# Where the activations and low weights of layer 1 stand in memory: other row distance, other gap between high and low part, shifted low weights

## The chip, the core and the metric

The kernel runs on one core of one Trainium2 chip. The metric is the time on the device, in microseconds (us), of one launch. One execution is also recorded by the hardware profiler; its time is given beside its span, which is the time from the first to the last instruction.

The engines are named as in the profile: PE is TensorE's matmul, PEld its weight load, DVE is VectorE, ACT is ScalarE, POOL is GpSimd, SP is the engine that issues most of the DMAs.

## The reference

A decoder with two layers on 16 meta tokens and 256 sequence tokens (272 in all), width 2048, 16 heads of 128, feed-forward width 8192, all in fp32:

```python
h = concatenate([meta, x])                       # 272 tokens
# layer 0: forgetting attention
a = rms_norm(h, norm_attn[0]); q, k, v, f = split(a @ fox_w_in)
h = h + forgetting_attention(q, k, v, cumsum(log_sigmoid(f + b))) @ fox_w_o
h = h + square(relu(rms_norm(h, norm_mlp[0]) @ w_up[0])) @ w_down[0]
# layer 1: stick-breaking attention over a shared K/V
k_s, v_s = split(rms_norm(h, kv_norm) @ w_kv)
q = rms_norm(h, norm_attn[1]) @ sb_w_q
h = h + stick_breaking_attention(q, k_s, v_s) @ sb_w_o
h = h + square(relu(rms_norm(h, norm_mlp[1]) @ w_up[1])) @ w_down[1]
return rms_norm(h, final_norm)[16:]
```

Nearly all the arithmetic is in the products with weight matrices: 96 blocks of 512 output features over 2048 input features, each.

## The kernel before

**Three products for one.** Activations are held feature-major: 128 partitions, 16 chunks of 128 features, and the tokens along the free axis. To keep fp32 accuracy with the faster float32r matmuls, every operand is split into a high part (rounded to float32r) and a low part (the rest). A product is then high x high + high x low + low x high, summed in PSUM.

**Activations.** `Split` (from line 119) makes a tile of 16 rows for one activation, one row for each chunk, with the high and the low part of the chunk in one row. The table `ROWS` (line 28) says, in words of 4 bytes, how far rows are apart, where the high part begins and where the low part begins. For layer 0, where all 272 tokens are needed (`t0` = 0), rows are 640 words (2560 bytes) apart, the high part begins at 48 (byte 192) and the low part at 368 (byte 1472). For layer 1 after the shared K/V (`t0` = 16, 256 tokens) rows are 576 words (2304 bytes) apart, the high part begins at word 16 (byte 64) and the low part follows right behind it at 272. `both` is the two parts of a row as one operand of 512 columns; it is used in layer 1 alone, since 2 x 272 columns do not fit into the 512 of one PSUM bank.

**Weights.** `gemm_group` (from line 182) multiplies one block of 512 output features. It goes over four quarters `kb` of the input features. For each it loads four chunks of weights (issued on SP's queue, two chunks to a DMA), and for each half of them line 217 makes the high weights `whi` on ScalarE and line 218 the low weights `wlo` on VectorE. There are four buffers of each. The tile `pad` of 128 bytes (line 115) puts the weight buffers, and the activation tiles behind them, at multiples of 256 bytes.

**Matmuls.** All are issued through `gemm_matmul` (from line 174), line 176 in the profile. Without `pairs` (layer 0 and the shared K/V) there are three matmuls of 272 columns for each chunk and each 128 output features: `whi` with high, `whi` with low, `wlo` with high. With `pairs` (layer 1's query and output projections and its MLP) there are two: `whi` with `both`, 512 columns, and `wlo` with the high part, 256 columns. In the first and last quarter the four output features' blocks come one after the other (four 512s, then four 256s); in the two middle quarters two chunks go with all four blocks (eight 512s, then eight 256s). A manual dependency from each matmul to the one before it pins this order, so no scheduler changes it. In one group of layer 1 there are 64 of each; there are 40 such groups, and in the last one a quarter of the products is done in the form of layer 0 (256 columns).

Lines 600 to 605 are matmuls of the stick-breaking attention, float32r as well, whose activations come in two pieces: 2 x 256 or 2 x 144 columns with a jump between them. Lines 305 and 306 multiply layer 0's activations with the 16 forget-gate weights (high and low, 32 columns).

Of the kernel before, what the change touches and what calls it, by code (L numbers as in the profile page):

```python
# [10 lines left out]
F32R = mybir.dt.float32r  # L11
# [4 lines left out]
P = 128  # L16
D = 2048
NC = D // P
M = 16
# [4 lines left out]
QSCALE = 1.0 / math.sqrt(P)  # L24
N_FF = 4


ROWS = {0: (640, 48, 368), M: (576, 16, 272)}
XROW = 640

G_A0, G_M0, G_KV, G_A1, G_M1, G_FIN = range(6)
# [3 lines left out]
def yoco_kernel(ctx: ExitStack, tc: tile.TileContext, hT_in, gains, b_f, w_f, w_qkv0, w_o0, w_up, w_dn,  # L35
# [7 lines left out]
    wspl = ctx.enter_context(tc.tile_pool(name="wspl", bufs=4))  # L43
# [75 lines left out]
    class Split:  # L119


        def __init__(self, label, t0):
            n = T - t0
            self.t0 = t0
            rows = xs.tile([P, NC * XROW + 64], F32R, tag="x", name=f"x_{label}")
            pitch, hi, lo = ROWS[t0]
            rows = rows[:, hi:hi + NC * pitch].rearrange("p (c t) -> p c t", c=NC)
            self.hi, self.lo = rows[:, :, :n], rows[:, :, lo - hi:lo - hi + n]
            self.both = rows[:, :, :2 * n]

    def split_chunk(sp, gi, c):

# [41 lines left out]
    def gemm_matmul(*args, **kw):  # L174

        ins = nc.tensor.matmul(*args, **kw).ins  # L176
        if queued and pinned[0]:
            tc.add_manual_dep(ins, queued[0].name, mybir.DependencyInfo(mybir.DependencyClass.NoSync,
                                                                        mybir.DependencyReason.DATA))
        queued[:] = [ins]  # L180

    def gemm_group(wblk, sp, t0, evac, before={}, after={}, load_x=None, pairs=False, apart=()):

        uid[0] += 1
        u = uid[0]
        accs = [pacc.tile([P, 512], F32, tag="acc", name=f"acc_{u}_{m}") for m in range(4)]  # L190
        n = T - t0
        for kb in range(4):
            src_w = wblk[kb].rearrange("p (k c) -> p k c", k=4)
            if kb in before:
                before[kb]()
            piece = 1 if load_x is not None and kb < 2 else 2
            raws = [wraw.tile([P, 2, 512], F32, tag="raw", name=f"raw_{u}_{kb}_{hf}") for hf in range(2)]
            for k0 in range(0, 4, piece):
                if load_x is not None:
                    load_x(range(4 * kb + k0, 4 * kb + k0 + piece))  # L200
                if load_x is not None and kb == k0 == 0:

                    for c0 in (0, 256):
                        nc.scalar.dma_start(raws[0][:, 0, c0:c0 + 256], src_w[:, 0, c0:c0 + 256])
                else:
                    nc.sync.dma_start(raws[k0 // 2][:, k0 % 2:k0 % 2 + piece], src_w[:, k0:k0 + piece])
            parts = []
            for hf in range(2):
                whi = wspl.tile([P, 2, 512], F32R, tag="whi", name=f"whi_{u}_{kb}_{hf}")
                wlo = wspl.tile([P, 2, 512], F32R, tag="wlo", name=f"wlo_{u}_{kb}_{hf}")  # L210
                boxes = [(o, piece, 0, 512) for o in range(0, 2, piece)]
                if load_x is not None and kb == hf == 0:
                    boxes[:1] = [(0, 1, 0, 256), (0, 1, 256, 512)]
                for o, no, c0, c1 in boxes:
                    src = raws[hf][:, o:o + no, c0:c1]
                    hp, lp = whi[:, o:o + no, c0:c1], wlo[:, o:o + no, c0:c1]
                    on_act = nc.scalar.activation(hp, src, AF.Copy)  # L217
                    on_dve = nc.vector.tensor_tensor(out=lp, in0=src, in1=hp.bitcast(F32), op=ALU.subtract)  # L218
                parts.append((whi, wlo))
            if kb in after:  # L220
                with tc.issue_after(on_act.ins), tc.issue_after(on_dve.ins):
                    after[kb]()


            if load_x is not None and kb == 0:
                runs = [([kc], range(4)) for kc in range(4)]
            elif kb in (0, 3):
                runs = [(range(4), [m]) for m in range(4)]
            else:
                runs = [(range(2 * hf, 2 * hf + 2), range(4)) for hf in range(2)]  # L230
            pinned[0] = load_x is None
            for kcs, ms in runs:
                paired = [m for m in ms if pairs and m not in apart]
                single = [m for m in ms if m not in paired]
                for kc in kcs:
                    for m in paired:
                        gemm_matmul(accs[m], parts[kc // 2][0][:, kc % 2, m * P:(m + 1) * P], sp.both[:, 4 * kb + kc],
                                    start=kb == kc == 0, stop=False)
                for kc in kcs:
                    for m in paired:  # L240
                        gemm_matmul(accs[m][:, :n], parts[kc // 2][1][:, kc % 2, m * P:(m + 1) * P],
                                    sp.hi[:, 4 * kb + kc], start=False, stop=kb == kc == 3)
                for m in single:
                    for kc in kcs:
                        wh, wl = (w[:, kc % 2, m * P:(m + 1) * P] for w in parts[kc // 2])
                        hi, lo = sp.hi[:, 4 * kb + kc], sp.lo[:, 4 * kb + kc]
                        gemm_matmul(accs[m][:, :n], wh, hi, start=kb == kc == 0, stop=False)
                        gemm_matmul(accs[m][:, :n], wh, lo, start=False, stop=False)
                        gemm_matmul(accs[m][:, :n], wl, hi, start=False, stop=kb == kc == 3)
                if kb == 3:  # L250
                    for m in ms:
                        evac(m, [accs[m][:, :n]] + ([accs[m][:, n:]] if m in paired else []))
# [18 lines left out]
    def load_x(chunks):  # L271
        c0, n = chunks[0], len(chunks)
        nc.sync.dma_start(hT[:, c0:c0 + n, :], hT_in[:, c0:c0 + n, :])
        if c0 == 0:
            nc.sync.dma_start(g_sb, gains)
        for c in chunks:
            split_chunk(xa, G_A0, c)
# [86 lines left out]
    for g in range(4):  # L364
# [11 lines left out]
        if g == 0:  # L376

            gemm_group(w_qkv0[0], xa, 0, lambda m, acc, qT=qT: nc.scalar.copy(qT[:, m, :], acc[0]),
                       after={kb: (lambda kb=kb: first_norm(kb)) for kb in range(4)}, load_x=load_x)
            gate_products()  # L380
            box["rstd"] = norm.finish()
            for m in range(4):
                evac_q(m, [qT[:, m, :]])
            forget_gates(box["rstd"])
        else:
            gemm_group(w_qkv0[3 * g], xa, 0, evac_q)
# [4 lines left out]
        def decays(j):  # L391

            for i, (o, n) in enumerate(((0, 144), (144, T))):
                nc.vector.scalar_tensor_tensor(out=s[:, j, o:o + n], in0=fk[:, j, :n],
                                               scalar=fq_sb[:, i, 4 * g + j:4 * g + j + 1],
                                               in1=maskA[:, o:o + n], op0=ALU.subtract, op1=ALU.add)

        gemm_group(w_qkv0[3 * g + 1], xa, 0, lambda m, acc: evac_kv(m, acc, kT),
                   after={j: (lambda j=j: decays(j)) for j in range(4)})

# [255 lines left out]
    a, y, t, rs = (fin[:, i, :] for i in range(4))  # L656
# [81 lines left out]
```

## Time and profile before

| | before |
|---|---|
| time, median of 3 runs | 2323.51 us (2322.72 to 2324.66) |
| profiled execution | 2323.63 us, span 2321.9 us |
| granted TensorE clock | 0.998 |
| PE busy | 2310.8 us (100%), 16486 instructions |
| DVE, ACT busy | 1350.6 us (58%), 1064.0 us (46%) |
| DMA | 412.00 MB, 177 GB/s on average |

Matmuls are pipelined: the next one starts before the one ahead has ended. The duration that the profile gives for one is therefore longer than the step from its start to the start of the next, and it is the steps that add up to the time.

### The profile page before, as it was taken

To read this page: it belongs to the slowest core of one execution; us is meant where nothing else is said; L and a number is where in the kernel's file an instruction comes from. 1 tells how busy PE (TensorE), PEld (TensorE's weight loads), DVE (VectorE), ACT (ScalarE), POOL (GpSimd) and SP (SyncE) were. 2 spreads that over 40 slices of the span, in tenths; PEclk is the share of its full clock that TensorE was granted. 3 is DMA by queue.
4 is the path that set the end of the run, shared out by engine and by line. 5 is a ranking of instruction groups with operands and counts; after the bars stand their busy time and mean duration, and the time that the engine had idled before them with its cause. 6 is when DMAs were issued, how large, how long until landed. Compare 5 with 4: busy or idle time off the path is not lost.

```text
span 2321.9 us, 39954 instructions
## 1 busy us (share of the span) xinstructions
PE 2310.8 (100%) x16486; PEld 2190.4 (94%) x16486; DVE 1350.6 (58%) x1923; ACT 1064.0 (46%) x1477; POOL 39.9 (2%) x58
## 2 busy tenths in 40 slices
PE   9999999999999999999999999999999999999998
PEld 9999999999999999999998999988888888888887
DVE  7665555655455455445566655567665665665665
ACT  6434344544344344344455444455544543543553
POOL 1000000000000000000000000000000000000000
PEclk9999999999999999999999999999999999999999
DMA  6544444455555455555556444455555555556553
GB/s 233 172 156 165 171 158 173 171 183 173 183 175 183 171 186 176 178 182 171 187 173 200 155 145 146 146 175 186 197 184 193 192 186 198 186 184 199 181 199 127
DMA packets 116630, 412.00 MB, mean 177 GB/s; under 512 B 13264, under 2 KB 16736, under 8 KB 116448
## 3 DMA queue, kind: packets, MB, share of 16 engines
q1 hardware_dynamic: 114560, 406.29, 51.4%
q10 hardware_dynamic: 1888, 3.16, 0.4%
q8 instruction: 129, 2.11, 0.4%
q14 instruction: 53, 0.43, 0.1%
HBM read 407.29 MB, written 2.11 MB: 176 GB/s over the span
## 4 chain that ended last, share of the span: by engine, by line
PE 99%; DMA 0%; DVE 0%; ACT 0%; issue 0%; DVEq 0%; SPq 0%; ACTq 0%
PE acc L176 95%; PE ps L406 0%; PE pza L585 0%; PE pv L339 0%; PE po L468 0%; PE po L624 0%; DMA raw<-w_qkv 0%; PE po L625 0%; PE pzb L586 0%; PE po L469 0%; DMA hT<-hT_in 0%; PE po L626 0%; DVE ob L680 0%; PE pf L306 0%; PE pf L305 0%; PE pta L600 0%
## 5 line engine op out<-in xcount | busy, mean ns | idle before, releaser
L218 DVE TENSOR_TENSOR wlo<-raw,whi 128x1024 fp32r<-128x1024 f32 (+1 forms) x773 | 931.5, 1217 | 746.8 <-ACT whi L217 745.2
L217 ACT ACTIVATE whi<-raw 128x1024 fp32r<-128x1024 f32 (+1 forms) x773 | 799.2, 1050 | 953.9 <-PE acc L176 877.4
L176 PE MATMUL acc<-x_u,whi 128*128 128x272 f32 (+2 forms) x3088 | 647.5, 321 | 0.0
L176 PE MATMUL acc<-x_m,whi 128*128 128x272 f32 (+1 forms) x3072 | 646.1, 322 | 0.0
L176 PEld LDWEIGHTS acc<-x_u,whi 128*128 128x128 f32 x3088 | 499.9, 188 | 26.7
L176 PEld LDWEIGHTS acc<-x_m,whi 128*128 128x128 f32 x3072 | 497.8, 188 | 27.4
L176 PE MATMUL acc<-x_u,wlo 128*128 128x272 f32 (+1 forms) x2048 | 445.9, 282 | 0.0
L176 PE MATMUL acc<-x_m,wlo 128*128 128x272 f32 (+1 forms) x2048 | 443.7, 282 | 0.0
L176 PE MATMUL acc<-x_a,whi 128*128 128x272 f32 (+1 forms) x1792 | 360.6, 306 | 0.4 <-ACT x_a L134 0.2
L176 PEld LDWEIGHTS acc<-x_u,wlo 128*128 128x128 f32 x2048 | 340.3, 188 | 15.7
L176 PEld LDWEIGHTS acc<-x_m,wlo 128*128 128x128 f32 x2048 | 339.5, 188 | 15.9
L176 PEld LDWEIGHTS acc<-x_a,whi 128*128 128x128 f32 x1792 | 284.4, 188 | 9.9 <-issue 0.7
L176 PE MATMUL acc<-x_a,wlo 128*128 128x272 f32 (+1 forms) x1024 | 254.5, 286 | 0.0
L176 PE MATMUL acc<-x_kv,whi 128*128 128x272 f32 x1024 | 194.1, 288 | 0.0
L176 PEld LDWEIGHTS acc<-x_a,wlo 128*128 128x128 f32 x1024 | 179.6, 188 | 4.9 <-issue 0.5
L176 PE MATMUL acc<-x_o,whi 128*128 128x272 f32 (+1 forms) x768 | 162.3, 322 | 0.0
L176 PEld LDWEIGHTS acc<-x_kv,whi 128*128 128x128 f32 x1024 | 160.6, 188 | 0.4
L176 PE MATMUL acc<-x_kv,wlo 128*128 128x272 f32 x512 | 147.3, 288 | 0.0
L256 DVE TENSOR_TENSOR hT<-acc,hT 128x256 f32<-128x256 f32 (+1 forms) x239 | 102.4, 428 | 71.4 <-PE acc L176 69.5
L176 PEld LDWEIGHTS acc<-x_o,whi 128*128 128x128 f32 x768 | 124.3, 188 | 6.8
L176 PE MATMUL acc<-x_o,wlo 128*128 128x272 f32 (+1 forms) x512 | 111.6, 283 | 0.0
L176 PEld LDWEIGHTS acc<-x_kv,wlo 128*128 128x128 f32 x512 | 96.5, 188 | 0.1
(226 smaller groups left out, 1040.0 us busy)
## 6 DMA issues: line engine op xcount, KB each, us to landing
raw<-w_up SPq DMA_DIRECT2D x256, 512.0 KB, 4.7
raw<-w_dn SPq DMA_DIRECT2D x256, 512.0 KB, 4.7
raw<-w_qkv SPq DMA_DIRECT2D x92, 512.0 KB, 3.8
raw<-w_o SPq DMA_DIRECT2D x64, 512.0 KB, 4.5
raw<-w_kv SPq DMA_DIRECT2D x64, 512.0 KB, 3.6
raw<-w_q SPq DMA_DIRECT2D x32, 512.0 KB, 4.6
fk<-f_dram ACTq DMA_DIRECT2D x4, 544.0 KB, 5.0
raw<-w_qkv SPq DMA_DIRECT2D x7, 256.0 KB, 4.8
```

The lines of the kernel that those rows point to most:

```text
L176: ins = nc.tensor.matmul(*args, **kw).ins
L217: on_act = nc.scalar.activation(hp, src, AF.Copy)
L218: on_dve = nc.vector.tensor_tensor(out=lp, in0=src, in1=hp.bitcast(F32), op=ALU.subtract)
L256: nc.vector.tensor_tensor(out=hT[:, c, t0:], in0=a, in1=hT[:, c, t0:], op=ALU.add)
```

## The change

Rows of all activations are 640 words (2560 bytes) apart, layer 1's too. In layer 1 the high part begins at byte 0 of its row, a multiple of 256, and the low part 304 words (1216 bytes) behind it, so that 192 bytes lie unused between the two and `both` is an operand of two pieces. The tiles of split weights grow from 2 x 512 to 2 x 576 words; in layer 1 (`pairs`) the low weights are put 16 words (64 bytes) into their tile. The two halves of a weight tile thus lie 2304 instead of 2048 bytes apart, in both layers. No instruction is added or taken away on any engine, and their order is the same.

```diff
-ROWS = {0: (640, 48, 368), M: (576, 16, 272)}
+ROWS = {0: (48, 368), M: (0, 304)}
 XROW = 640
...
             rows = xs.tile([P, NC * XROW + 64], F32R, tag="x", name=f"x_{label}")
-            pitch, hi, lo = ROWS[t0]
-            rows = rows[:, hi:hi + NC * pitch].rearrange("p (c t) -> p c t", c=NC)
-            self.hi, self.lo = rows[:, :, :n], rows[:, :, lo - hi:lo - hi + n]
-            self.both = rows[:, :, :2 * n]
+            hi, lo = ROWS[t0]
+            rows = rows[:, hi:hi + NC * XROW].rearrange("p (c t) -> p c t", c=NC)
+            d = lo - hi
+            self.hi, self.lo = rows[:, :, :n], rows[:, :, d:d + n]
+
+            self.both = rows[:, :, :2 * d].rearrange("p c (i t) -> p c i t", i=2)[:, :, :, :n]
...
-                whi = wspl.tile([P, 2, 512], F32R, tag="whi", name=f"whi_{u}_{kb}_{hf}")
-                wlo = wspl.tile([P, 2, 512], F32R, tag="wlo", name=f"wlo_{u}_{kb}_{hf}")
+                whi, wlo = (wspl.tile([P, 2, 576], F32R, tag=f"w{x}", name=f"w{x}_{u}_{kb}_{hf}") for x in ("hi", "lo"))
+                whi, wlo = whi[:, :, :512], wlo[:, :, 16:528] if pairs else wlo[:, :, :512]
```

## The prediction

> **What bounds the kernel now.** I read the page's busy table first, then the waits of TensorE, the chain of work that ended last, and the timeline of TensorE in layer 1.
>
> ```profile
> PE 2310.8 (100%) x16486; PEld 2190.4 (94%) x16486; DVE 1350.6 (58%) x1923; ACT 1064.0 (46%) x1477; POOL 39.9 (2%) x58
> PE 99%; DMA 0%; DVE 0%; ACT 0%; issue 0%; DVEq 0%; SPq 0%; ACTq 0%
> PE acc L176 95%; PE ps L406 0%; PE pza L585 0%; PE pv L339 0%; PE po L468 0%; PE po L624 0%; DMA raw<-w_qkv 0%; PE po L625 0%; PE pzb L586 0%; PE po L469 0%; DMA hT<-hT_in 0%; PE po L626 0%; DVE ob L680 0%; PE pf L306 0%; PE pf L305 0%; PE pta L600 0%
> ```
>
> TensorE is busy throughout and 95% of the chain is the matmuls of line 176. So the time is the number of matmuls times the distance from one start to the next. The "mean ns of one" in the page (393 for 512 columns) is longer than that distance, because matmuls overlap; distances have to be read from start times. The chain's long pieces give them:
>
> ```profile
> 442.52 757.05 PE acc L176 x6112
> ...
> 1610.15 693.91 PE acc L176 x4020
> ```
>
> The first piece is layer 0, where every matmul has 272 columns: 757.05 / 6112 = 123.9 ns each. The second is layer 1, where matmuls of 512 columns (high weights on both halves of a row) and of 256 (low weights on the high half) come in equal numbers: 172.6 ns on average. The timeline separates the two (start, length in us; the next row's start minus this one's, divided by the count, is the distance):
>
> ```profile
> 1798.40 1.09 PE L176 MATMUL acc<-x_m,whi 128*128 128x512 f32 x4
> 1799.33 0.62 PE L176 MATMUL acc<-x_m,wlo 128*128 128x256 f32 x4
> ...
> 1803.94 2.00 PE L176 MATMUL acc<-x_m,whi 128*128 128x512 f32 x8
> 1805.78 1.10 PE L176 MATMUL acc<-x_m,wlo 128*128 128x256 f32 x8
> 1806.72 2.00 PE L176 MATMUL acc<-x_m,whi 128*128 128x512 f32 x8
> 1808.56 1.11 PE L176 MATMUL acc<-x_m,wlo 128*128 128x256 f32 x8
> 1809.51 2.00 PE L176 MATMUL acc<-x_m,whi 128*128 128x512 f32 x8
> 1811.34 1.07 PE L176 MATMUL acc<-x_m,wlo 128*128 128x256 f32 x8
> 1812.25 1.99 PE L176 MATMUL acc<-x_m,whi 128*128 128x512 f32 x8
> ```
>
> Runs of 512 columns stand 230 (1.84 / 8), 230, 228.8 ns apart, and 232.5 in the run of four. Runs of 256 stand 117.5, 118.8 and then 113.8 ns apart. The same instruction on the same kind of data takes two speeds, without an idle moment. That is the only thing in this profile which a change of addresses alone could move.
>
> **What changes, and what does not.** On every engine the built program has the same instructions in the same order as before; only addresses and the shape of three operands differ. Nothing is removed and no wait is added. Byte positions within 256 are what I call residues; weight and activation tiles start at residue 0 in both kernels.
>
> *Layer 0* keeps its rows (2560 bytes apart, both parts at residue 192). Its weight tiles grow from 4096 to 4608 bytes, so the second half lies 2304 instead of 2048 bytes on, still residue 0. In the runs above, activations move by 2304 bytes and weights by 512 with no visible step, so I put this at nothing. If it did matter, 10,752 matmuls would pay: 1 ns each is 10.8 us.
>
> *The weight splits* (lines 217 and 218) write two pieces of 512 instead of one of 1024. Bound: nothing, up to two separate pieces, from these rows:
>
> ```profile
> L217 ACT ACTIVATE whi<-raw 128x1024 fp32r<-128x1024 f32 x764 | 794.0, 1055 | 950.1 <-PE acc L176 877.4 <-DVE hT L256 54.1 <-DMA fqm_sb<-f_dram 6.1
> L217 ACT ACTIVATE whi<-raw 128x512 fp32r<-128x512 f32 x7 | 4.4, 624 | 1.5 <-DMA raw<-w_qkv 1.5
> ```
>
> That is 2 x 624 - 1055 = 193 ns at most on ScalarE, eight times per group of 128 matmuls (22.17 us, start 1798.40 to the next group at 1820.57): 1.5 us, while ScalarE sits idle 877 us in all because it waits for TensorE to free weight buffers. Hidden. Without that cover it would be 764 x 0.19 = 147 us.
>
> *Layer 1's low part* moves from right behind the high part to 1216 bytes behind it. The 512-column operand becomes two pieces of 256 with a jump between. There are 2544 such matmuls (the by-form rows: 1024 + 1008 + 256 + 256). Only the stick-breaking matmuls of lines 600 to 605 already read two pieces:
>
> ```profile
> 1322.50 0.39 PE L601 MATMUL pta<-el,ntri_r 128*128 128x512 f32 x1
> 1322.73 0.30 PE L602 MATMUL pta<-eh,nones_r 128*128 128x288 f32 x1
> 1322.86 0.30 PE L603 MATMUL pta<-el,nones_r 128*128 128x288 f32 x1
> 1323.00 0.30 PE L605 MATMUL ptb<-el,ntri_r 128*128 128x288 f32 x1
> 1323.13 0.42 PE L176 MATMUL acc<-x_kv,whi 128*128 128x272 f32 x2
> ```
>
> Their pieces start at residues that neither version of the rows uses. Three matmuls of 2 x 144 columns take 400 ns (1322.73 to 1323.13), 133.3 each. In one piece, 288 columns should take 123.9 plus 16 columns at (230 - 116.4) / 256 = 0.44 ns, or 130.9. So a jump costs about 2.4 ns. Line 601, 512 columns in two pieces, takes 230 ns, like the contiguous ones: a jump for nothing. Upper end: line 600's 240 ns (1320.53 to 1320.77 in the same timeline), 10 ns over 230. I take 2.4, from three in succession, and keep 0 and 10: 2544 x 2.4 = +6.1 us (0 to +25).
>
> *The residues of layer 1* go from 64 for everything on the activation side and 0 for weights to: high activations 0, low activations 192, high weights 0, low weights 64. For the 256-column matmuls the activations now stand 64 before the weights, modulo 256 the same difference (192) that layer 0 has throughout. Layer 0's 123.9 ns for 272 columns, less 16 x 0.44, is 116.9 for 256; layer 1's mean now is 116.4 (the group's 22.17 us is 64 x 346.4, less 64 x 230). So for these 2592 matmuls I expect +0.5 ns, within the rounding: 0. The bounds are the fastest and slowest runs seen, 113.8 and 118.8: -6.7 to +6.2 us. For the 512s the runs of four in this stretch span 227.5 (1799.79 to 1800.70) to 232.5: -6.4 to +6.4 us, taken at 0 because no row has activations and weights at one residue.
>
> A rule of the Trainium skill speaks against any effect of the weights' place: "TensorE: Matmul & The Clock Gate", Part 2, says that matmul operand and weight load have independent read ports and don't take bandwidth from each other. The trace bears it out where weights are small: lines 305 and 306 load 32 columns instead of 128, and ten of them take 1.25 us (31.69 to 32.94), 125 ns each against 123.9 with full weights. By that rule the residue term is zero, and the sum has the jump alone.
>
> **Sum.** The profiled execution took 2323.63 us (span 2321.9, 1.7 around it), 0.1 above the median of 2323.51. 2323.6 + 6.1 = 2329.7, say **2330**. A measurement of this kernel can tell about 0.2% (4.6 us) from no change.
>
> **The rivals.**
>
> *Faster: the new residues put every run on its fast speed.* For: the two speeds exist at one and the same instruction and shape, so what decides is how activations' and weights' reads fall against each other, and the change sets that anew in each of the three pairings. Against: layer 0's residues differ from layer 1's and cost the same per column. All 256s at 113.8 and all 512s at 227.5: 2592 x 2.6 + 2544 x 2.5 = 13.1 us, 2310; it shows as faster once it beats the jump by 4.6 us. Chance 0.30. The same page gives N / 2.4 + 2.5 ns as the bare distance between matmuls; an estimate by it, 215.8 and 109.2 ns, would make the most that could be gained 55 us.
>
> *No difference.* The jump is free, as in line 601, and the residues do nothing: 2323 to 2325. Also the case if lock-in at the two speeds is reached whatever the addresses. Chance 0.15.
>
> *Much slower: equal residues collide.* Now high activations and high weights both start at residue 0, which no matmul of line 176 has in the kernel before. If each 512 meets the next weight load head on, the nearest price is line 600's 10 ns: 25 us; with all 256s at 118.8, another 6: 2349 to 2355. It becomes decisive above 4 ns per matmul. Chance 0.20.
>
> *The forecast*, jump paid and residues about even, 2328 to 2338: 0.35.
>
> **Numbers.** Faster by over 0.2% is 0.30; within 0.2% is the second rival, 0.15; slower is 0.35 + 0.20 = 0.55. The range runs from 2309, just below the gain of 13, to 2348, which leaves out the farther part of the collision and any gain beyond the fast speeds. Cases of both signs hold most of it; the forecast's own range is 2328 to 2338.
>
> **What would show it.** Right: the 512-column runs of layer 1 stand 2 to 3 ns farther apart, the 256s near 116 to 117, layer 0's chain piece still gives 123.9, TensorE has no new idle time. The residues matter if runs of 256 come all at one speed. The forecast is wrong if the 512s fall below 229, if layer 0 moves, or if ScalarE's wait for TensorE shrinks to nothing.

## The result, and the profile after

The changed kernel takes 2316.13 us (2315.55 to 2316.42), the kernel before 2323.47 us in the same series: ratio 0.9968, 95% interval [0.9956, 0.9979]. It is faster by 7.3 us, where I forecast 6.5 us slower. The time lies inside the stated range, in the part of it that the first rival holds; the forecast itself missed the sign.

The page of the changed kernel, busy times (line 176 is now line 177):

```profile
PE 2303.4 (100%) x16486; PEld 2183.1 (94%) x16486; DVE 1350.1 (58%) x1923; ACT 1064.1 (46%) x1477; POOL 40.8 (2%) x58
```

TensorE is as full as before and issues as many instructions; it is busy 7.4 us less. The chain's long pieces say in which layer:

```profile
442.66 756.95 PE acc L177 x6112
...
1608.68 688.23 PE acc L177 x4020
```

Layer 0's piece was 757.05 us and is unchanged. Layer 1's was 693.91 and is 5.7 us shorter. The rest of the gain is in layer 1's shorter pieces. The timeline of TensorE in the same group of layer 1 (start, length in us):

```profile
1795.29 1.08 PE L177 MATMUL acc<-x_m,whi 128*128 128x512 f32 x4
...
1800.78 2.00 PE L177 MATMUL acc<-x_m,whi 128*128 128x512 f32 x8
1802.62 1.07 PE L177 MATMUL acc<-x_m,wlo 128*128 128x256 f32 x8
1803.53 2.00 PE L177 MATMUL acc<-x_m,whi 128*128 128x512 f32 x8
...
1817.26 1.08 PE L177 MATMUL acc<-x_m,whi 128*128 128x512 f32 x4
```

A run of eight 512s takes 1800.78 to 1802.62, 230 ns each, as before. A run of eight 256s takes 1802.62 to 1803.53, 113.8 ns each by these rounded starts; by the unrounded ones of the trace 113.3, and so in all but three of the layer's 469 runs of 256. Before, a third of the runs stood at 113.3 by unrounded starts and the others at 117.5 to 118.5, and the mean was 116.4. The whole group takes 1795.29 to 1817.26, 21.97 us instead of 22.17. Forty groups at 0.2 us are 8 us, about the result.

The weight splits are still hidden, and ScalarE still waits for TensorE nearly as long as before (873.8 us in its row for line 218, against 877.4).

### The profile page after: what moved, and what is told of

Same layout as the page of the kernel before. It is cut to its first block, busy times and chain, and to the rows that moved or that the text cites. A ratio compares the mean times of both kernels' runs of the same rounds, so it can differ in the third digit from the quotient of the medians.

```text
span 2314.5 us, 39954 instructions
## 1 busy us (share of the span) xinstructions
PE 2303.4 (100%) x16486; PEld 2183.1 (94%) x16486; DVE 1350.1 (58%) x1923; ACT 1064.1 (46%) x1477; POOL 40.8 (2%) x58
## 4 chain that ended last, share of the span: by engine, by line
PE 99%; DVE 0%; DMA 0%; ACT 0%; issue 0%; SPq 0%; DVEq 0%; ACTq 0%
PE acc L177 96%; PE ps L407 0%; PE pza L586 0%; PE pv L340 0%; PE po L469 0%; PE po L625 0%; PE pzb L587 0%; PE po L626 0%; PE po L470 0%; DMA g_sb<-gains 0%; PE po L627 0%; DVE ob L681 0%; PE pf L306 0%; PE pf L307 0%; PE pta L601 0%; PE pta L602 0%
## 5 line engine op out<-in xcount | busy, mean ns | idle before, releaser
L218 ACT ACTIVATE whi<-raw 128x1024 fp32r<-128x1024 f32 (+1 forms) x773 | 799.1, 1050 | 948.0 <-PE acc L177 873.8
```

## The experiments

What had to be explained: why the 256s all run at 113.3 ns now, and why the 512s' mean didn't move although they got a jump and new starts. All starts below are in bytes modulo 256. "Speed" is the distance from the start of one matmul to that of the next. Where the text names two rows it is worked out from their rounded starts, which is good to about 1 ns in a run of eight and 2.5 ns in a run of four; elsewhere, and in all means, it is from the unrounded starts of the trace.

The theories as they stood when the first runs were made: **A**, that the difference between the start of the activations and that of the low weights decides (192, where it was 64); **B**, that a start of the high activations at a multiple of 256 decides; **C**, that the 512s ahead, with their jump, leave TensorE in a state that decides how the 256s go.

### One part of the change alone

The changed kernel without the displacement of the low weights:

```diff
-                whi, wlo = whi[:, :, :512], wlo[:, :, 16:528] if pairs else wlo[:, :, :512]
+                whi, wlo = whi[:, :, :512], wlo[:, :, :512]
```

> The changed kernel with its rows (2560 bytes apart, high part at residue 0, low part at 192), but the low weights back at residue 0. Theory A (the 256-column matmuls run at their fast speed when the high activations stand 192 past the low weights, modulo 256): the difference is now 0, so runs of 256 fall back to a mixture near 116.4 ns and the time to about 2323 us. Theory B (the start of the activations at a multiple of 256 decides, whatever the weights): all runs of 256 stay at 113.3 ns, about 2316 us. Theory C (the 512s ahead, with their jump, leave TensorE in a state that decides): also 113.3 ns and 2316 us.

Measured: 2332.88 us, ratio to the kernel before 1.0039 [1.0024, 1.0054]. Its timeline in layer 1:

```profile
1809.39 1.12 PE L177 MATMUL acc<-x_m,wlo 128*128 128x256 f32 x8
1810.35 2.00 PE L177 MATMUL acc<-x_m,whi 128*128 128x512 f32 x8
```

The 256s stand 120 ns apart (1809.39 to 1810.35; 119.4 in the mean of the layer), where the slow runs of the kernel before had 118.5 at most; the 512s are nearly where they were, at 230.6 in the mean. So 64 bytes on the low weights, in this setting, are worth 16.8 us. All three theories missed: A expected a mixture near 116.4 ns, B and C expected 113.3. B falls, and so does C in the form above, since the 512s kept their starts and their jump. What is left of it is a wider **C**, which the later runs test: the matmuls ahead leave TensorE's reads in a position that is kept, so that the 512s' starts have a part in the 256s' speed, beside the 256s' own.

The other part alone, the kernel before with low weights displaced by 64:

```diff
-                wlo = wspl.tile([P, 2, 512], F32R, tag="wlo", name=f"wlo_{u}_{kb}_{hf}")
+                wlo = wspl.tile([P, 2, 576], F32R, tag="wlo", name=f"wlo_{u}_{kb}_{hf}")
+                wlo = wlo[:, :, 16:528] if pairs else wlo[:, :, :512]
```

(the tile of `whi` grows likewise, and is used from its start).

> The kernel before with its rows (2304 bytes apart, both parts at residue 64 and contiguous), and the low weights of layer 1 displaced by 64 bytes; weight tiles as in the change. Theory A: the difference of high activations and low weights becomes 0 instead of 64, not 192: no gain of 7 us, somewhere within 2320 to 2330. Theories B and C: nothing changes, 2323.5 us, runs of 256 at 113.8 to 118.8 as before. If it gives 2316, the weights' place alone is the cause.

Measured: 2326.62 us, 1.0014 [1.0004, 1.0023]. Activations and low weights now both start at 64, and over half of the 256s go at 119 to 121 ns, some at 113; the mean is 117.8. Equal starts are slow in both runs, but here not for all. A had 2320 to 2330 us for this run, B and C no change.

### The same difference, no jump

High part at 192 and the low part right behind it, low weights at 0: A's difference of 192 without a jump.

```diff
-ROWS = {0: (48, 368), M: (0, 304)}
+ROWS = {0: (48, 368), M: (48, 304)}
-                whi, wlo = whi[:, :, :512], wlo[:, :, 16:528] if pairs else wlo[:, :, :512]
+                whi, wlo = whi[:, :, :512], wlo[:, :, :512]
```

> Rows of layer 1 2560 bytes apart, high part at residue 192 and the low part right behind it (no jump), low weights at residue 0. The difference of activations and weights is 192 for all three pairings, as in layer 0. Theory A: runs of 256 all at 113.3 ns, about 2316 us. Theory B: mixed as before, 2323 us. Theory C: no jump, mixed as before, 2323 us.

Measured: 2324.83 us, 1.0005 [0.9996, 1.0014]. In its timeline

```profile
1804.37 2.02 PE L177 MATMUL acc<-x_m,whi 128*128 128x512 f32 x8
1806.23 1.07 PE L177 MATMUL acc<-x_m,wlo 128*128 128x256 f32 x8
1807.15 2.02 PE L177 MATMUL acc<-x_m,whi 128*128 128x512 f32 x8
```

the 256s do go at 113.3 (all but the first of a run, which brings their mean to 114.3), as A had it, but the 512s take 232.5 ns (1804.37 to 1806.23; mean 232.4) instead of 230, and eat the gain. No theory had that: A expected 2316 us, and B and C, whose 2323 us is near, expected the 256s mixed as before. The version without a jump is the slower, but its starts differ too, so this run doesn't price the jump; two of the sweeps below do.

### A sweep of starts, matmuls alone

```python
for rh, rl, rw in product(range(4), repeat=3):   # starts of high part, low part, low weights
    # twice: eight 512s (whi, both parts), then eight 256s (wlo, high part)
```

> Not the decoder: only matmuls on copies of inputs, in runs of 24 to 48, with their places swept (letters a to p are starts 0, 16, ... 240 bytes past a multiple of 256; o, a, b, c are 0, 64, 128, 192), and the output is a copy of the input. Lines by group: 256 columns by start; 256 columns by start and by the weights' start; 272 columns; 512 contiguous; layer 1's pattern of eight 512s and eight 256s by starts of high part, low part and low weights; layer 0's pattern of three by the same. Theory A: in the 256-column groups the distance depends on the difference alone, 113.3 ns at 192. Theory B: it depends on the activations' start alone. Theory C: groups of 256 alone all have one speed, and in the pattern it depends on the low part's start. If neither place matters, all groups of a shape have one distance: 116.4, 123.9, 230.

The names of its groups give the three starts, o, a, b and c for 0, 64, 128 and 192. Three groups with the high part at 0:

```profile
261.12 1.11 PE L90 MATMUL pair_ooa<-x,wl 128*128 128x256 f32 x8
262.06 2.00 PE L85 MATMUL pair_ooa<-x,wh 128*128 128x512 f32 x8
...
325.63 1.12 PE L90 MATMUL pair_oco<-x,wl 128*128 128x256 f32 x8
326.59 2.00 PE L85 MATMUL pair_oca<-x,wh 128*128 128x512 f32 x8
328.43 1.07 PE L90 MATMUL pair_oca<-x,wl 128*128 128x256 f32 x8
329.34 2.00 PE L85 MATMUL pair_oca<-x,wh 128*128 128x512 f32 x8
```

The second 256 row of `pair_oco`, the starts of the first experiment, takes 325.63 to 326.59, 120 ns each; `pair_oca`, the changed kernel's, 113.8; `pair_ooa`, which differs from it only in where the low part lies, 117.5. The 256s never read the low part. That speaks for C and against A. A 512 and a 256 together took 343.4 ns with the changed kernel's starts, the best of the 64, and 350.0 with the low part at 128, which the next experiment puts into the kernel.

The sweep also had groups of 256s alone, with no 512s between, and there both expectations missed. A had 113.3 ns at a difference of 192: of the four such groups one took 113.4, and the other three, the changed kernel's 0 and 64 among them, 117.7 to 117.8. C had one speed for all: the 16 groups went from 113.4 to 120.2, with the four of equal starts at 119.7 to 120.2. So the 256s' own starts have a part in it. But the same 256s at 0 and 64 that take 117.8 ns alone take 113.4 behind the 512s of `pair_oca`.

### The low part's start alone, in the kernel

The changed kernel with the low part at 128 instead of 192. The 256s' own operands stay where they were.

```diff
-ROWS = {0: (48, 368), M: (0, 304)}
+ROWS = {0: (48, 368), M: (0, 288)}
```

> The changed kernel with the low part 1152 instead of 1216 bytes behind the high one (residue 128 instead of 192); high part, low weights and the matmuls of 256 columns keep their addresses. Theory A (high activations 192 past the low weights decide): nothing changes for the 256s, 113.3 ns, and about 2316 us. Theory C (the 512s before leave a state that decides): the sweep's group with these starts has 117.9 and 232.1 ns instead of 113.3 and 230.0, so 40 groups x 64 x 6.7 ns = 17 us more, about 2333 us.

Measured: 2333.55 us, 1.0041 [1.0026, 1.0056], as C had it.

```profile
1810.10 1.11 PE L177 MATMUL acc<-x_m,wlo 128*128 128x256 f32 x8
1811.04 2.02 PE L177 MATMUL acc<-x_m,whi 128*128 128x512 f32 x8
```

The 256s fall back to 117.5 ns (1810.10 to 1811.04; mean 117.9) although nothing of theirs moved, and the 512s go to 232.1 in the mean. A falls: the difference of 64 between activations and low weights isn't enough. 17.4 us lie between two kernels that differ in where a low part lies.

### A miss: low weights displaced by 128

The kernel before, its rows untouched, `wlo[:, :, 32:544]` in layer 1.

> The kernel before with its rows (2304 bytes apart, contiguous, residue 64), low weights displaced by 128 bytes instead of 64. Theory A: the difference is 64 - 128, which is 192 modulo 256, so all 256s go to 113.3 ns: 2592 x 3.1 = 8 us less, about 2316 us. Theory C: needs the order of speeds in the 512s; the sweep's group with these starts (with a jump between the parts) has 229.4 and 113.3 to 114, so about 2316 us as well, while the weights displaced by 64 gave 2326.6. Rival (only a multiple of 256 for the high part helps): 2323 us or slower.

Measured: 2329.49 us, 1.0024 [1.0014, 1.0033]; both theories missed. Two stretches of one group:

```profile
1797.82 0.63 PE L176 MATMUL acc<-x_m,wlo 128*128 128x256 f32 x4
1798.29 1.10 PE L176 MATMUL acc<-x_m,whi 128*128 128x512 f32 x4
...
1814.14 1.07 PE L176 MATMUL acc<-x_m,wlo 128*128 128x256 f32 x8
1815.05 2.00 PE L176 MATMUL acc<-x_m,whi 128*128 128x512 f32 x8
```

In half of the runs of eight the 256s have the fast speed (1814.14 to 1815.05, 113.8), in those of four it's lost (1797.82 to 1798.29, 117.5). One set of starts has two speeds, and the kernel's order of matmuls changes from one to the other. The lost time is the 512s', though: the 256s' mean is 116.6 ns, as in the kernel before, while that of the 512s went from 229.9 to 232.0, 2544 x 2.1 = 5.3 us.

### Where the slow speed comes from

A finer sweep: starts in steps of 16 bytes, and the 256s by themselves with weights of 128 columns ("full") and of 32 ("short") at 0, 64, 128 and 192 (o, a, b, c), the activations at 0.

```python
nc.tensor.matmul(a[i % 4][:n, :256], wl[:, k, at:at + n], xs(k, 0, 256))   # n = 128, then 32
```

> Again only matmuls on copies of inputs, the output a copy. First: 256 and 512 columns from start 0 against weights at 0, 64, 128, 192, with loads of 128 columns (full) and of 32 (short). If the two speeds come from the reads of activations meeting the reads of weights, the short loads are free of the weights' place and all stand near 113 and 226.7 ns or less; if the activations alone cause them, short and full loads differ nowhere. Then, in steps of 16 bytes: layer 1's pattern with joined parts (start of the row, of the low weights), with a jump (low part, low weights; high part at 0), and layer 0's pattern of three (both parts together and low weights; low part alone and low weights). Theory C: joined parts at 64 with low weights at 128 give about 343 ns for a pair, at 64 and 0 about 346; nothing in layer 0's pattern is far below 123.35.

```profile
24.94 5.91 PE L85 MATMUL full_o<-x,wl 128*128 128x256 f32 x48
30.69 5.82 PE L85 MATMUL full_a<-x,wl 128*128 128x256 f32 x48
...
47.70 11.10 PE L90 MATMUL fullw_o<-x,wl 128*128 128x512 f32 x48
...
91.99 5.61 PE L85 MATMUL short_o<-x,wl 128*32 128x256 f32 x48
97.44 5.60 PE L85 MATMUL short_a<-x,wl 128*32 128x256 f32 x48
...
113.76 11.28 PE L90 MATMUL shortw_o<-x,wl 128*32 128x512 f32 x48
```

With full weights the four places take 120.0, 117.9, 118.6 and 117.8 ns (24.94 to 30.69 is 48 matmuls). With short ones all four take 113.3, once the first two matmuls are past. So 113.3 is what 256 columns take when few weights are loaded beside them; in these groups what is above it comes with the load of the next 128 columns of weights, and where these lie plays a part in it.

For 512 columns (`fullw` and `shortw`) the expectation missed. Short weights should have brought them to 226.7 ns or less; they took 230.6 to 231.8 at the four places, while full weights at 0 settle at 226.7 after the first ten (over all 48, 11.10 us against 11.28). So a smaller load doesn't make every matmul fast, and what holds the 512s back here stays open.

The same sweep prices the jump by itself. Sixteen pairs of its groups have both parts at 0 and the low weights at the same place, once with the low part right behind the high one and once 256 bytes farther on. In 15 of the pairs the 512s differ by at most 0.13 ns; in the pair with low weights at 0, whose joined group is the first after the short weights, by 0.9. A jump of 256 bytes costs nothing there.

### Row distance and tile size

The kernel before with the changed kernel's row distance and weight tiles, but its own starts (high at 64, low right behind, low weights at 0): `ROWS = {0: (48, 368), M: (16, 272)}`.

> The changed kernel with layer 1's parts where they were before (high part at residue 64, low part right behind it, low weights at 0): what is left of the change is the row distance of 2560 and the weight tiles of 2 x 576 words. Theory C (only starts modulo 256 matter): 2323.5 us, the same two speeds in the same places as before. If row distance or tile size had a part in the gain, 2316 to 2321.

Measured: 2323.43 us, 0.9999 [0.9990, 1.0009]. These two parts of the change do nothing.

### The long sweep, and a second miss

Starts in the kernel's own order of matmuls, 128 to a group.

> Only matmuls on copies of inputs, the output a copy: the combinations that were quickest in the fine sweep, now each in the order of a whole group of the kernel (layer 0's 192 matmuls; layer 1's 128 twice). Theory C: a start that looks good in eight and eight can lose in four and four, since each switch between 512 and 256 columns may leave the fast state; low part at 192 with low weights at 64 gives 22.0 us for a group, joined parts at 64 with weights at 0 give 22.17, joined at 64 with weights at 128 give more than that. Layer 0: the present starts give 123.4; the quickest of the fine sweep 122.3 if they hold over a group.

Layer 1: the changed kernel's starts took 21.97 us for a group, the best of those tried; those of the kernel before 22.09; those with low weights displaced by 128 took 22.31, which is the miss above. Five pairs of groups that differ in a jump of 256 bytes alone took the same to 0.01 us. Layer 0: its present starts (192, 192, 0) took 123.33 ns per matmul, as in the kernel, and one set, 192, 48 and 32 for high part, low part and low weights, 122.22. I put that set into the kernel:

```diff
-ROWS = {0: (48, 368), M: (0, 304)}
+ROWS = {0: (48, 332), M: (0, 304)}
-                whi, wlo = whi[:, :, :512], wlo[:, :, 16:528] if pairs else wlo[:, :, :512]
+                whi, wlo = whi[:, :, :512], wlo[:, :, 16:528] if pairs else wlo[:, :, 8:520]
```

> The changed kernel, with two starts of layer 0 changed as well, where no row of before or after differed: the low part of an activation row of 272 columns starts at a residue of 48 bytes modulo 256 (it was 192, as the high part's), and the low weights lie 32 bytes further on. Nothing else is edited. In the sweep with the kernel's order of matmuls these starts gave 122.2 ns for a matmul of 272 columns, and the present ones 123.3. Theory C, that a lock between reads of activations and reads of weights decides, and that the order of matmuls before keeps or loses it: the order is the sweep's, so 10,752 matmuls of layer 0 take 1.1 ns less each, 11.8 us, and the time is 2304 us (2302 to 2308). Theory A, that only the difference between the high activations and the low weights decides, and 192 is its good value: in layer 0 that difference goes from 192 to 160, so no gain, 2316 us or more (to 2330, if the matmuls on low weights go to 124.5 ns). If the lock that the sweep found is lost at the ends of groups in the kernel, the time lies between, near 2310 us.

Measured: 2326.79 us, 1.0014 [1.0005, 1.0023]. The starts that gave 122.22 in the sweep give 124.45 here, in nearly every group of the MLP. Layer 1 kept its 113.3. The time lies in A's range (2316 to 2330); C had 2304.

### One set of starts, several lasting speeds

The next kernel varied layer 0's starts from group to group in the kernel itself, with a table of starts by activation (`START`, in words) and one of the low weights' places by group (`WLO`).

> The sweep of layer 0's starts inside the kernel: the changed kernel, with the starts of its two-layer MLP in layer 0 varied from group to group (a group is 192 matmuls of 272 columns, some 23.7 us at 123.3 ns). For the 16 groups on the tile x_m the low activations start at a residue of 48 bytes modulo 256, and the low weights move by 16 bytes from one group to the next; the four groups on each tile x_u have four places of the low weights and one pair of starts (high, low) per tile: (192, 208), (192, 112), (144, 144) and (192, 192) bytes. Theory A, that the starts alone decide: a group has the same time here as with the same starts elsewhere; the group with starts 192, 48 and 32 bytes takes 124.4 ns per matmul, as in the run with these starts in all of layer 0, and no group beats 123.3. Theory C, that one set of starts has two or more steady speeds and what ran before decides which: that group may take 122.2 ns, as in the long sweep, since it now comes after a group with other starts; and some of the sets that fell back in the long sweep to 124.4 come out at 122.2 or 123.3. The whole time is a mean over 32 groups of such sets, near 2322 us (2316 to 2330), and is not the point.

Time 2325.51 us. The set above took 124.46 here too, which by itself is what A said (from here on A is the wider theory that the starts of all operands alone decide). But the set 192, 208, 176, at 124.46 in the long sweep, took 122.23 in this kernel, through its group of 192 matmuls; A said that none would beat 123.3. That group came after one with the low weights at 160. Three kernels then used this one set in layer 0:

```diff
+START = {x: (48, 372) for x in ("m0", "u0_0", "u0_1", "u0_2", "u0_3")}
+WLO = {"m0": (44,), "u0_0": (40, 44), "u0_1": (44,), "u0_2": (40, 44), "u0_3": (44,)}
...
-            hi, lo = ROWS[t0]
+            hi, lo = START.get(label, ROWS[t0])
+            self.wlo = list(WLO.get(label, [16 if t0 else 0]))
...
+        at = sp.wlo.pop(0) if len(sp.wlo) > 1 else sp.wlo[0]
-                whi, wlo = whi[:, :, :512], wlo[:, :, 16:528] if pairs else wlo[:, :, :512]
+                whi, wlo = whi[:, :, :512], wlo[:, :, at:at + 512]
```

> The changed kernel with one set of starts in the whole MLP of layer 0 (32 groups of 192 matmuls, none at all changed elsewhere): high activations at 192 bytes modulo 256, low ones at 208, low weights at 176, which took 122.23 ns per matmul in one group of the sweep in place and 124.46 in the long sweep. The first group on the first and on the third tile x_u has its low weights at 160 bytes, since the fast group came after such a one. Theory C with one more assumption, that a speed once found is kept from group to group: 122.2 ns from the second group on the first x_u to the end of the layer, 27 groups, 27 x 192 x 1.1 = 5.7 us less, and the four or five groups before at up to 124.5, 1.1 us more: 2311.5 us (2310 to 2314). Theory A, that starts alone decide and this set is simply fast: all 32 at 122.2, 2309.4. Theory C without the assumption, the fast speed lost at a stage's end as with the run that changed all of layer 0: most groups at 124.5, 32 x 192 x 1.1 = 6.8 us more, 2323 us.

The same without the detour, `(44,)` in place of `(40, 44)`:

> The run before this one without its detour: high activations at 192, low ones at 208, low weights at 176 bytes modulo 256 in all 32 groups of layer 0's MLP, and no group with the low weights at 160. Theory C, that a speed is kept from group to group until something changes the starts: the first four groups went at 124.45 ns per matmul with these starts, and nothing now comes that moves them off it, so all 32 stay at 124.45: 27 x 192 x 2.2 = 11.5 us more than the run with the detour, 2323.8 us (2322 to 2325). Rival D, that the change from tile x_m to tile x_u (another activation, another place) gave the switch and the detour had no part: from the first x_u on all at 122.2, 2311.5 us (2310 to 2313).

And with the set in all of layer 0, and a detour at the first group of each of four activations:

> The run with the detour, the three starts (192, 208 and 176 bytes) now in all of layer 0 and the shared K/V, 56 groups, with one group on low weights at 160 bytes as the first on each of the tiles x_a, x_o, x_m and x_kv. Theory C, with the detour as what brings the fast speed: 122.2 ns in 52 groups and 124.8 in the four of the detour; against the changed kernel's 123.33 that is 52 x 192 x 1.11 = 11.1 us less and 4 x 192 x 1.5 = 1.1 us more, 2306 us; attention matmuls between the groups of x_a may lose the speed there, so 2305 to 2310. Rival D, that the detour has no part, gives no reason for the fast speed in the first tiles: what the sixteen groups of x_m and x_u showed from the first x_u on stays (2312), and the groups added on x_a, x_o and x_kv and the first on x_m go at 124.4, 24 x 192 x 1.1 = 5 us more, 2317 us.

| | with detour | without | all of layer 0 |
|---|---|---|---|
| time, us | 2312.24 | 2322.51 | 2335.41 |
| ratio to the kernel before | 0.9950 [0.9934, 0.9967] | 0.9995 [0.9985, 1.0004] | 1.0050 [1.0035, 1.0065] |
| MLP's first groups at these starts, ns | 124.45 | 124.45 | 126.67 |
| after the first x_u's first group, ns | 122.22 | 124.45 | 126.67 |

The chain's piece of layer 0 in the kernel with the detour, then without it, and with the set in all of layer 0:

```profile
442.76 752.72 PE acc L181 x6112
```

```profile
443.23 763.62 PE acc L181 x6112
```

```profile
440.50 776.91 PE acc L181 x6112
```

The first piece holds the layer's MLP: the same instructions at the same starts take 752.72, 763.62 or 776.91 us, while layer 1's piece has 688.23 in all three. In the first kernel the groups before the detour go at 124.45 ns, all those from the group behind it on at 122.22, over 600 us (the second detour costs one group at 124.8, and the fast speed comes back). Without the detour 124.45 stays to the end; the change of activation alone does nothing, so rival D falls. That is C. Its size for the third kernel was a miss: there the groups behind the detour on x_m went at 126.67, and that stayed. C says that a speed is kept; it didn't say which one a detour leads to.

The kernel with the detour, 2312.24 us, beats both: layer 0's piece is 4.2 us shorter than the changed kernel's, and layer 1 has the same gain.

## Why the prediction was wrong

*What bounds the kernel* was right: TensorE's distances between starts, and the two speeds of the 256s as the one thing that addresses could move.

*Layer 0, nothing; weight splits, hidden:* right (757.05 and 756.95 us; ScalarE's wait for TensorE 873.8 us). The price of 123.9 ns was a little high: the last 11 us of that piece are layer 1's first matmuls, 32 of them of 512 columns. By starts a matmul of layer 0 takes 123.3, before and after; that shifts the price of the 256s below by 0.6 ns and leaves its conclusion. Row distance and tile size have no part, as the run with these two alone shows.

*The jump, +6.1 us:* mis-sized; it is about 0, as the pairs in the two sweeps show, which differ in a jump of 256 bytes alone. The 512s' mean in the kernel is 230.0 ns with jump and new starts and was 229.9. Line 601's 230 ns, which I named and passed over, was the nearer row, since it had 512 columns. The 133.3 ns that I chose came from 2 x 144 columns.

*The residues of the 256s, 0:* this is the step that failed. I worked out that the difference of 192 was "the same difference (192) that layer 0 has throughout", took layer 0's time per column as its price, and got +0.5 ns. Measured: 116.4 to 113.3, 2592 x 3.1 = 8.0 us less. That runs of 256 come all at one speed is what the prediction itself named as the sign that the starts matter. The reasoning took a distance between matmuls to be a property of two starts. The runs show it isn't: with its starts untouched, a 256 went from 113.3 to 117.5 when the 512s ahead had their low part elsewhere, and in layer 0, which served as the price, another set of starts has three speeds, 122.2 to 126.7, by what ran before. What could be known is the fast end of my bounds: it came for all runs. It lies a little beyond the stated -6.7 us, because 113.8 was read from rounded starts; by unrounded ones a third of the runs stood at 113.3 already. Why these starts give that speed stays open.

*The residues of the 512s, 0:* the number is right, 230.0 against 229.9, but in part by luck. The single distances did change, from 225 to 236 ns before to 228 to 232 after, and the means of other starts went from 229.7 to 232.4 in the kernels above.

*The rivals.* The first, every run on its fast speed, came true for the 256s alone: 2310 was for both. The collision at equal starts didn't come for the 512s, though high part and high weights both start at 0; equal starts are bad for the 256s instead (120 ns in the first experiment), in a place where the change avoids them.

*The rule of the Trainium skill*, "TensorE: Matmul & The Clock Gate", Part 2, that weight loads and matmul operands don't take bandwidth from each other, would make the weights' place indifferent. In the 256s that fits where weights have 32 columns (113.3 ns at every place). With 128 columns the place matters in these float32r matmuls: 117.8 to 120.0 ns alone, and 16.8 us between two kernels that differ in the low weights' start. The rows that I had put beside it, lines 305 and 306, load 32 columns, and so could not speak against it.

*Sum:* -8.0 for the 256s, +0.3 for the 512s' 0.1 ns, 0 for the jump; the span shrank by 7.4 us.

## What to carry to other kernels

Where TensorE is full and a trace shows one instruction at two distances without idle time, try other starts of moving operand and weights modulo 256: it costs no instruction, and here 64 bytes were worth 17 us of 2330 in one setting and 3 us the other way in another. Judge it in the kernel itself: sets that were good in a sweep failed in the kernel twice here, the second one after a sweep in the kernel's own order over a whole group. Where the speed depends on what ran before, a group by itself doesn't settle it. Price such a change by the fastest and slowest run of the same instruction, not by another instruction's mean.

## What was not expected of the hardware

- A run of matmuls settles on a lasting speed, and one set of starts can have three: 122.22, 124.45 and 126.67 ns for 272 columns, each held over hundreds of microseconds. Which one comes depends on what ran before; a group with the low weights 16 bytes elsewhere switched it.
- The speeds are mostly stepped: nearly all groups of layer 0 stood at 122.22, 123.33, 124.45, 125.55 or 126.67 ns, which is 3.33 ns more from one to the next for three matmuls (`whi` on high, `whi` on low, `wlo` on high). A few in the long sweep and in the kernels with varied starts stood between, at 123.7, 124.8, 125.0 or 125.2.
- What position of the reads it is that is kept, why a load of 128 columns slows some 256s, and what slows the 512s where the load is small, stays open: the runs show its effects on time, and no view of the profile shows the reads themselves.
